# A macaron decoder layer on one core: reversed queries, a sixth weight split behind a copy, spaced squares, running-sum transfers in a new place, and a group add on VectorE

## The chip, the cores and the metric

The kernel runs on one core of a Trainium2 chip. The metric is the device time of one execution in microseconds (us), from the runtime's measurement; the profile, taken from a separate execution of the same program, gives the span from the first to the last instruction. Before the change the median of three runs is 1312.29 us (1311.63 to 1313.32).

The engines are named as the profile names them: PE is the matrix engine (PEld its weight loads), DVE is VectorE, ACT is ScalarE, POOL is GpSimd, and SP issues transfers. ACT and POOL issue transfers too.

## The reference

One layer for a sequence of 512 tokens with 1024 features, in float32:

```
x = x + 0.5 * swiglu(rms_norm(x), ffn1)          # 1024 -> 2 x 2816 -> 1024
x = x + mixer(rms_norm(x))                       # two head groups share projections
x = x + cross_attention(rms_norm(x), mem)        # 4 heads over 256 memory rows
x = x + 0.5 * swiglu(rms_norm(x), ffn2)
out = rms_norm(x) * gain
```

The mixer has 16 state-space (SSD) heads in 4 groups, with a causal convolution, a chunked scan over 4 chunks of 128 tokens, a gate and a norm for each group of 256 features; and 8 differential-attention heads, each with two query-key pairs of 64 features. Their logits get a bias by relative position before a causal softmax:

```
rel  = k_pos[None, :] - q_pos[:, None]
bias = rel_bias[rel_bucket(rel)]                 # depends on k_pos - q_pos alone
logits = q k^T * scale + bias                    # masked where rel > 0
w = softmax(logits[0]) - lam * softmax(logits[1]);  out = w v
```

## The kernel before

**Arithmetic.** Every matrix product is done in a reduced 32-bit format with operands split into a high and a low part: ACT copies the value into the high part (`wh` for weights, L155; with a factor L159), DVE subtracts to get the low part (`wl`, L156; with a factor L160), and PE runs three products (high by high, high by low, low by high). PE is fed by these splits everywhere, and each split of a 128 x 1024 weight tile must be done before the product that uses it. The weight tiles come from a pool with three buffers each for `wh` and `wl` and six for the raw tile `wr`, so a split may also have to wait until an earlier product has released its buffer.

**FFN blocks.** Each FFN is worked in three parts of the hidden dimension ("thirds"). The input projection of a pair of hidden tiles is a 2 x 2 block product done with seven products in place of eight: the function `quad` (L270). It runs the products `11`, S1, S2, `12`, S3, S4 and `22` of 24 matmuls each (2.88 us), into three accumulators `qa`, `qe`, `qb` (`a_ps`, `e_ps`, `b_ps` in the code; L243 issues the matmuls). Between them ACT copies `qa` into `qb` (L287 or L292), `qe` into `p` (L295) and `qb` into `u` (L302), and DVE forms the sums of weights that S2 and `22` need (L297 to L307, where they aren't ready in memory) and `qe - u` (L303). S3 adds into `qb`, so it cannot begin before `u` has been copied out of it. Seven splits of weights feed the seven products; the split for S4 (`w3`, the sixth) comes ahead of that product. The projected activations go through the gate (L450, L453), and a gated pair is combined into `s31` and `s24` (L212 to L214), which are split too (`s31h`, `s31l`, `s24h`, `s24l`) for the output product.

The output projection of a third is `out_blocks` (L1271): the same seven products, in parts of one or two tiles (`part`), into `oa`, `oe`, `ob` (L1300 issues the matmuls, L1311 updates the residual `x`). In the first FFN the sums of weights are not in memory: the function `added` fetches a block through SP and has POOL issue a transfer that adds a second block onto it in place (L1320); `t2` fetches a third block and DVE adds it (L1330); and `t4` has POOL add one more block onto the running sum with a transfer (L1341). In the last third, where `by_dma` is set, all running sums are done so. The raw tile of the first part of S3 is called `gate` there.

**What sets the order.** A scheduler sets the order of PE, DVE and ACT at build time. A class `Order` interleaves the generators of the dense work with spawned chains by estimated times; `yield` gives way to the other chains, and its number is the estimated time until the chain goes on. SP and POOL issue in program order. The helper `behind(list)` makes an instruction come after those listed on the same engine; it adds no wait between engines. An engine executes its instructions strictly in order, so an instruction that waits holds back everything behind it on its engine.

**Attention.** `queries_keys` projects one head's queries and keys and splits them (`split("q", pq, -1.0)` writes `qh` on ACT and `ql` on DVE). The bias of a head is a Toeplitz matrix. The kernel computes one row of it for each head in memory (`rel_d`, 8 rows of 640 values), copies this row 128 times into a second memory tensor `rel_z` with rows one longer (`expand_bias`, L640: two transfers from ACT, six from SP), and then reads it back shifted by one for each partition (`ask_bias`, L738). `head` adds it to the scores in the instruction at L776, and at the end transposes the output into `pot` and splits it into `yah` and `yal` (`split("ya", pt, wsub)`), the operands of the mixer's output projection `pm`, which L863 adds onto `x`.

**SSD groups.** At the end of each of the four groups ACT squares the two gated tiles (`ysq`, L1003), POOL adds the two (L1005), PE sums over the partitions (`pn`), and a chain of small steps (`nv` on DVE, then `ncol`, `ch`, `cl` and `ndiag` on POOL, `nrow` on PE) makes the norm's factors. POOL's queue also holds transfers that build weight sums for the second FFN in memory (L1266).

**The last squares.** Before the second FFN the residual is squared tile by tile on ACT with the row sum accumulated (`junk`, L554, four tiles last), and from the sums the norm's row is made, which the first gates of FFN2 need.

Of the kernel before, what the change touches and what calls it, by code (L numbers as in the profile page):

```python
# [100 lines left out]
def body(tc, a, dbg=None):  # L101
# [81 lines left out]
    @contextmanager  # L183
    def behind(ins):
        with ExitStack() as after:
            for i in ins:
                after.enter_context(tc.issue_after(i))
            yield
# [71 lines left out]
    def quad(xs, src, ready, fresh=False):  # L260
# [40 lines left out]
        u2 = s2("u2")  # L301
        S.activation(u2, b_ps, AF.Copy)  # L302
        V.tensor_tensor(e_ps, e_ps, u2, ALU.subtract)  # L303
# [6 lines left out]
        V.tensor_tensor(c22, p5, b_ps, ALU.subtract)  # L310
        yield from add_product(e_ps, split_w(m3), xs, S4, False)
        yield from add_product(b_ps, split_w(t4), xs, "22", False)
# [283 lines left out]
    rel_d = dram.tile([8, RW], F32, name="rel_d")  # L596
    rel_z = dram.tile([8, P, RW + 1], F32, name="rel_z")

# [18 lines left out]
    def prepare():  # L617
# [14 lines left out]
        hot.clear()  # L632
        yield 6.0
        for hd in range(2):
            with behind(list(recent)):
                expand_bias(S, hd)
            yield 4.0

    def expand_bias(queue, hd):
        queue.dma_start(rel_z[hd, :, :RW], rel_d[hd : hd + 1].to_broadcast([P, RW]))  # L640

# [94 lines left out]
    def ask_bias(hd):  # L736
        biases[hd] = s2("bias")
        S.dma_start(biases[hd], bass.AP(rel_z.tensor, rel_z.offset + hd * P * (RW + 1) + P - 1, [[RW, P], [1, T]]))  # L738

    def queries_keys(hd):  # L740
        if hd == 0:
            ask_bias(0)
        if hd < 7:
            ask_bias(hd + 1)
        if hd < 6:
            expand_bias(nc.sync, hd + 2)
        pq = acc("pq")
        yield from proj(pq, load_w(a["wq"][hd]), h)
        q = split("q", pq, -1.0)
        pk = acc("pk")  # L750
# [4 lines left out]
    def head(hd, q, kq, bias):  # L755
# [93 lines left out]
        for b in range(4):  # L849
            transpose(pt[:, b * P : (b + 1) * P], on[:, b])  # L850
        ya[hd] = split("ya", pt, wsub)
        dump(f"ya_{hd}", ya[hd][0])
# [59 lines left out]
    def group(g, bt, ct, xs, zs):  # L912
# [87 lines left out]
        for j in range(2):  # L1000
# [3 lines left out]
            sq.append(q_)  # L1004
        G.tensor_tensor(sq[0], sq[0], sq[1], ALU.add)  # L1005
        yield W["gq"] + (1.2 if g == 2 else 0.0)
# [262 lines left out]
    def out_blocks(blocks, sums, g, col4, ncol4, each=None, finale=None, clean=True, n=None, by_dma=False):  # L1269
# [109 lines left out]
        for t in range(2):  # L1379
            update(t, 0, a_ps[t])  # L1380
        yield from product(b_ps, sums[1], S3)
        for part in t_raw if by_dma else ():
            t4(part)
        for t in range(2):
# [79 lines left out]
    def turn_last():  # L1464
        yield from turn(1, summed=True)
        od.spawn(row_from(st_2, 8.0), 3.0)

# [91 lines left out]
```

## Time and profile before

| | us |
|---|---|
| median of three runs | 1312.29 |
| profiled execution, its own time | 1312.46 |
| its span, first to last instruction | 1310.7 |
| PE busy | 1287.7 |
| DVE busy | 970.1 |
| ACT busy | 707.8 |
| POOL busy | 127.1 |
| last matmul ends, from the start of the span | 1301.4 |

The profiled execution takes 1.8 us more than its span. PE is busy for all but 23 us of the span: 1.4 us pass before its first matmul, 9.3 us after its last, and the rest lies in gaps of 0.1 to 1.6 us between matmuls. So a change that leaves PE's own work as it is can only move these gaps, or make new ones. The names on both sides of an arrow in the rows below are the program's tiles, and the text in square brackets says how long an engine sat idle before an instruction and which instruction on another engine ended that wait.

### The profile page before, as it was taken

The page shows a single profiled execution, that of the slowest core. Times are in us where ns is not written, and L with a number is a line of the kernel's source. Part 1 is how long each engine was busy: PE and PEld are TensorE (multiplying, and loading weights), DVE is VectorE, ACT ScalarE, POOL GpSimd, SP SyncE. Part 2 cuts the span into 40 slices and gives each one's busy share as a digit, 9 for nine tenths or more (in the row PEclk, how much of TensorE's full clock was granted, in tenths as well). Part 3 has the DMA queues.
Part 4 walks back from the last instruction along what each step waited for, and adds up shares of the span by engine and source line. Part 5 has one row for each costly group of instructions (what it writes and reads, how often), then busy time and mean ns, then how long its engine had stood idle before and what let it go on. Part 6 is the DMA issues. An engine that isn't in the chain of part 4 may idle for free.

```text
span 1310.7 us, 20079 instructions
## 1 busy us (share of the span) xinstructions
PE 1287.7 (98%) x7709; PEld 1123.3 (86%) x7709; DVE 970.1 (74%) x1538; ACT 707.8 (54%) x1208; POOL 127.1 (10%) x153
## 2 busy tenths in 40 slices
PE   9999999999999999999999999999999999999997
PEld 7879998997787778777788878888889999989995
DVE  6977897797775676557867686645668878877886
ACT  7545564565754564346645465434365646555564
POOL 0001010001010011101003022020001000000000
PEclk9999999999999999999999999999999999999999
DMA  9367777776984434763466548684139876656652
GB/s 339 94 171 182 203 192 212 223 200 187 291 294 146 137 65 131 256 171 105 92 185 174 177 138 239 191 222 126 66 100 272 207 232 179 189 194 180 188 200 94
DMA packets 70415, 237.38 MB, mean 181 GB/s; under 512 B 8288, under 2 KB 9792, under 8 KB 69968
## 3 DMA queue, kind: packets, MB, share of 16 engines
q1 hardware_dynamic: 54064, 182.87, 41.1%
q0 software_dynamic: 13168, 45.67, 19.4%
q10 hardware_dynamic: 3088, 7.56, 1.6%
q8 instruction: 60, 0.98, 0.3%
q14 instruction: 35, 0.29, 0.1%
HBM read 233.92 MB, written 50.91 MB: 217 GB/s over the span
## 4 chain that ended last, share of the span: by engine, by line
PE 59%; issue 11%; DVE 3%; ACT 2%; DMA 1%; POOL 1%; POOLq 0%; ACTq 0%; DVEq 0%
PE pm L146 10%; PE qb L243 8%; PE qe L243 5%; PE qa L243 5%; PE pxbc L146 4%; PE ob L1300 4%; PE pcq L146 3%; PE pz L146 3%; PE oe L1300 2%; PE oa L1300 2%; PE pcv L146 2%; PE pq L146 2%; PE pv L146 1%; PE pk L146 1%; DMA gate<-in_f1b 1%
## 5 line engine op out<-in xcount | busy, mean ns | idle before, releaser
L155 ACT ACTIVATE wh<-wr 128x1024 fp32r<-128x1024 f32 (+1 forms) x323 | 328.4, 1020 | 355.7 <-issue 75.6
L156 DVE TENSOR_TENSOR wl<-wr,wh 128x1024 fp32r<-128x1024 f32 (+1 forms) x323 | 377.8, 1173 | 142.4 <-ACT wh L155 136.1
L777 ACT ACTIVATE ec<-ec,mn 128x512 f32<-128x512 f32 (+3 forms) x64 | 35.3, 554 | 33.7 <-DVE mn L776 33.7
L146 PE MATMUL pxbc<-hnh,wh 128*128 128x512 f32 x128 | 52.6, 411 | 0.0
L146 PE MATMUL pxbc<-hnh,wl 128*128 128x512 f32 x128 | 50.2, 393 | 0.0
L146 PE MATMUL pxbc<-hnl,wh 128*128 128x512 f32 x128 | 50.2, 392 | 0.0
L243 PE MATMUL qb<-s31h,wh 128*128 128x256 f32 x152 | 43.2, 284 | 3.2 <-ACT u L302 3.2
L243 PE MATMUL qb<-s24h,wh 128*128 128x256 f32 x152 | 43.1, 284 | 1.3 <-ACT qb L287 1.3
L243 PE MATMUL qa<-h11h,wh 128*128 128x256 f32 x152 | 43.1, 283 | 0.0
L243 PE MATMUL qa<-hmh,wh 128*128 128x256 f32 x152 | 43.0, 283 | 0.0
L243 PE MATMUL qa<-hml,wh 128*128 128x256 f32 x152 | 43.0, 283 | 0.0
L243 PE MATMUL qe<-s24h,wh 128*128 128x256 f32 x152 | 43.0, 283 | 0.0
L243 PE MATMUL qe<-s24l,wh 128*128 128x256 f32 x152 | 43.0, 283 | 0.0
L243 PE MATMUL qe<-s24h,wl 128*128 128x256 f32 x152 | 43.0, 283 | 0.0
L243 PE MATMUL qb<-hmh,wh 128*128 128x256 f32 x152 | 43.0, 283 | 0.0
L243 PE MATMUL qb<-hml,wh 128*128 128x256 f32 x152 | 43.0, 283 | 0.0
L243 PE MATMUL qb<-hmh,wl 128*128 128x256 f32 x152 | 43.0, 283 | 0.0
L243 PE MATMUL qa<-h11h,wl 128*128 128x256 f32 x152 | 43.0, 283 | 0.0
L243 PE MATMUL qb<-s24l,wh 128*128 128x256 f32 x152 | 43.0, 283 | 0.0
L243 PE MATMUL qb<-s24h,wl 128*128 128x256 f32 x152 | 43.0, 283 | 0.0
L243 PE MATMUL qa<-h11l,wh 128*128 128x256 f32 x152 | 43.0, 283 | 0.0
L243 PE MATMUL qa<-hmh,wl 128*128 128x256 f32 x152 | 43.0, 283 | 0.0
(457 smaller groups left out, 4169.9 us busy)
## 6 DMA issues: line engine op xcount, KB each, us to landing
wr<-in_f2q SPq DMA_DIRECT2D x44, 512.0 KB, 4.3
wr<-in_f1q SPq DMA_DIRECT2D x40, 512.0 KB, 4.4
wr<-in_f1b SPq DMA_DIRECT2D x25, 512.0 KB, 5.3
isum<-in_f2q SPq DMA_DIRECT2D x22, 512.0 KB, 5.2
wr<-isum SPq DMA_DIRECT2D x22, 512.0 KB, 5.1
wsum<-in_f2b SPq DMA_DIRECT2D x20, 512.0 KB, 6.2
wr<-wsum SPq DMA_DIRECT2D x20, 512.0 KB, 4.7
wr<-in_f1q POOLq DMA_DIRECT2D x16, 512.0 KB, 5.9
```

The source lines that it names most:

```text
L146: newest_mm[:] = [nc.tensor.matmul(out, w, x, start=start, stop=stop).ins]
L155: S.activation(hi, src, AF.Copy),
L156: V.tensor_tensor(lo, src, hi.bitcast(F32), ALU.subtract),
L243: newest_mm[:] = [nc.tensor.matmul(out, a_[:, wc], b_, start=first and f == 0 and kp == 0 and j == 0, stop=kp == n - 1 and j == 2, skip_gr ...
L777: S.activation(ec[:, :n], ec[:, :n], AF.Exp, bias=mn, scale=-1.0, accum_out=sm[c][:, i : i + 1])
L1300: newest_mm[:] = [nc.tensor.matmul(ps, a_[:, ts], b_[:, ws], start=first and k == 0 and j == 0, stop=k == n - 1 and j == 2, skip_group_che ...
```

## The change

Five things change, and no matmul is added or removed (PE has the same 7333 rows of the program; two short pieces of it stand in another place).

- **Sixth split behind a copy.** In every `quad`, the split of the weights for S4 (`w3`) is now ordered behind the copy `u` on ACT.
- **Reversed queries.** The queries are reversed within each block of 128 as they are split (`backwards`: the split reads its source with a step of -1), and the bias is read from `rel_d` with overlapping rows in one transfer; `rel_z` and its eight expanding transfers go. The attention output is turned back when `pot` is split into `ya`. 8 `qh`, 8 `ql`, 8 `yah` and 8 `yal` instructions read PSUM backwards.
- **Last squares spaced.** The four last squares are a chain of their own, 2 us apart by the planner's estimate and each behind the newest split of weights, in place of four in a row.
- **Running sums' transfers.** In the last third of the first FFN, the `t4` transfers are written inside the product S3, behind that product's first split, and no longer after it.
- **Group squares added on VectorE.** The add at L1005 moves from POOL to DVE, four times.

```diff
--- before.py
+++ after.py
@@ -299,7 +299,7 @@
         if not ready:
             V.tensor_tensor(t4, t2, m2, ALU.add)
         u2 = s2("u2")
-        S.activation(u2, b_ps, AF.Copy)
+        copy = S.activation(u2, b_ps, AF.Copy)
         V.tensor_tensor(e_ps, e_ps, u2, ALU.subtract)
         yield from add_product(a_ps, split_w(m2), xs, "12", False)
         w7 = split_w(m7)
@@ -308,7 +308,9 @@
         yield from add_product(b_ps, w7, xs, S3, False)
         c22 = s2("c22")
         V.tensor_tensor(c22, p5, b_ps, ALU.subtract)
-        yield from add_product(e_ps, split_w(m3), xs, S4, False)
+        with behind([copy.ins]):
+            w3 = split_w(m3)
+        yield from add_product(e_ps, w3, xs, S4, False)
         yield from add_product(b_ps, split_w(t4), xs, "22", False)
         yield (a_ps, b_ps), (e_ps, c22)
 
@@ -594,7 +596,6 @@
     wsub = cp.tile([P, 1], F32, name="wsub")
     dskh = cp.tile([P, 8], F32, name="dskh")
     rel_d = dram.tile([8, RW], F32, name="rel_d")
-    rel_z = dram.tile([8, P, RW + 1], F32, name="rel_z")
 
     def lambdas():
         lamv = cp.tile([P, 4, 64], F32, name="lamv")
@@ -630,14 +631,6 @@
         for i in range(2):
             S.dma_start(rel_d[:, i * H : (i + 1) * H], hot[i][:8])
         hot.clear()
-        yield 6.0
-        for hd in range(2):
-            with behind(list(recent)):
-                expand_bias(S, hd)
-            yield 4.0
-
-    def expand_bias(queue, hd):
-        queue.dma_start(rel_z[hd, :, :RW], rel_d[hd : hd + 1].to_broadcast([P, RW]))
 
     def bc_c(t):
         return t[:, None, :].to_broadcast([P, 4, 16])
@@ -735,18 +728,20 @@
 
     def ask_bias(hd):
         biases[hd] = s2("bias")
-        S.dma_start(biases[hd], bass.AP(rel_z.tensor, rel_z.offset + hd * P * (RW + 1) + P - 1, [[RW, P], [1, T]]))
+        S.dma_start(biases[hd], bass.AP(rel_d.tensor, rel_d.offset + hd * RW, [[1, P], [1, T]]))
+
+    def backwards(t):
+        n = t.free_size()
+        return bass.AP(t.tensor, t.offset + P - 1, [list(t.ap[0]), [P, n // P], [-1, P]])
 
     def queries_keys(hd):
         if hd == 0:
             ask_bias(0)
         if hd < 7:
             ask_bias(hd + 1)
-        if hd < 6:
-            expand_bias(nc.sync, hd + 2)
         pq = acc("pq")
         yield from proj(pq, load_w(a["wq"][hd]), h)
-        q = split("q", pq, -1.0)
+        q = split("q", backwards(pq), -1.0)
         pk = acc("pk")
         yield from proj(pk, load_w(a["wk"][hd]), h)
         kq = split("k", pk)
@@ -848,7 +843,7 @@
         pt = aux("pot")
         for b in range(4):
             transpose(pt[:, b * P : (b + 1) * P], on[:, b])
-        ya[hd] = split("ya", pt, wsub)
+        ya[hd] = split("ya", backwards(pt), wsub)
         dump(f"ya_{hd}", ya[hd][0])
 
     wcv = []
@@ -1002,7 +997,7 @@
             q_ = s2("ysq")
             S.activation(q_, yz[j], AF.Square)
             sq.append(q_)
-        G.tensor_tensor(sq[0], sq[0], sq[1], ALU.add)
+        V.tensor_tensor(sq[0], sq[0], sq[1], ALU.add)
         yield W["gq"] + (1.2 if g == 2 else 0.0)
         pn = aux("pn", (P, 4))
         for b in range(4):
@@ -1378,9 +1373,14 @@
         later.clear()
         for t in range(2):
             update(t, 0, a_ps[t])
-        yield from product(b_ps, sums[1], S3)
-        for part in t_raw if by_dma else ():
-            t4(part)
+        for n, _ in enumerate(product(b_ps, sums[1], S3)):
+            if n == 0:
+                first_split = list(recent)
+            elif n == 4 and by_dma:
+                with behind(first_split):
+                    for part in t_raw:
+                        t4(part)
+            yield
         for t in range(2):
             update(t + 2, 1, b_ps[t], -1)
         if finale is None:
@@ -1462,8 +1462,15 @@
             yield from out_blocks(a[f"f2b{c}"], wsum[c], g, col4, ncol4, *((norm, store) if at_end else (None, None)), clean=c == 0)
 
     def turn_last():
-        yield from turn(1, summed=True)
-        od.spawn(row_from(st_2, 8.0), 3.0)
+        yield from turn(1)
+        od.spawn(row_of_last(), 4.0)
+
+    def row_of_last():
+        for k in range(4, KT):
+            with behind(list(newest)):
+                squared(k, x[k])
+            yield 2.0
+        yield from row_from(st_2, 3.0)
 
     od.add(turn_last())
     od.add(ffn2())
```

ScalarE around the sixth split, in the first FFN, where a gated pair (`s31`, `s24`) is split between a group's products; `wh_2768` belongs to S3, `wh_2802` to S4 and `wh_2830` to `22`. Before:

```order
L155 ACTIVATE wh_2768<-wr_2618 128x1024
L295 ACTIVATE p_488_2685<-qe_2622 128x512
L155 ACTIVATE wh_2802<-wr_2614 128x1024
L155 ACTIVATE s31h_2710<-s_491_2705 128x512
L155 ACTIVATE wh_2830<-wr_2611 128x1024
L302 ACTIVATE u_495_2733<-qb_2623 128x512
L155 ACTIVATE s24h_2749<-s_492_2706 128x512
L155 ACTIVATE gh_2784<-th_2603 128x512
L155 ACTIVATE wh_2880<-wr_2865 128x1024
```

After, the same place (the tile numbers are one lower):

```order
L155 ACTIVATE wh_2767<-wr_2617 128x1024
L295 ACTIVATE p_488_2684<-qe_2621 128x512
L155 ACTIVATE s31h_2709<-s_491_2704 128x512
L302 ACTIVATE u_495_2732<-qb_2622 128x512
L155 ACTIVATE s24h_2748<-s_492_2705 128x512
L155 ACTIVATE wh_2801<-wr_2613 128x1024
L155 ACTIVATE gh_2783<-th_2602 128x512
L155 ACTIVATE wh_2829<-wr_2610 128x1024
L155 ACTIVATE wh_2879<-wr_2864 128x1024
```

The copy `u` moved ahead of the splits for S4 and for `22`, which stood ahead of it before. The same happens once more, in the next but one group, 42 us later; in the changed kernel's other groups, in both FFNs, the sixth split stands behind `u` as well.

ScalarE at the start of the second FFN: the last tiles of `x`, the four squares `junk`, and the first group's copies and splits (`qb<-qa` is the copy ahead of S2). Before:

```order
L155 ACTIVATE s31h_9789<-s_2038_9783 128x512
L155 ACTIVATE s24h_9793<-s_2039_9784 128x512
L554 ACTIVATE junk_9818,squares_230<-x_119 128x512
L554 ACTIVATE junk_9821,squares_230<-x_121 128x512
L554 ACTIVATE junk_9824,squares_230<-x_123 128x512
L554 ACTIVATE junk_9827,squares_230<-x_125 128x512
L287 ACTIVATE qb_9844<-qa_9842 128x512
L295 ACTIVATE p_2068_9908<-qe_9843 128x512
L155 ACTIVATE wh_9942<-wr_9835 128x1024
L155 ACTIVATE wh_9978<-wr_9837 128x1024
L155 ACTIVATE wh_10015<-wr_9840 128x1024
```

After:

```order
L155 ACTIVATE s31h_9780<-s_2038_9774 128x512
L155 ACTIVATE s24h_9784<-s_2039_9775 128x512
L556 ACTIVATE junk_9872,squares_230<-x_119 128x512
L155 ACTIVATE wh_9925<-wr_9818 128x1024
L287 ACTIVATE qb_9827<-qa_9825 128x512
L295 ACTIVATE p_2062_9887<-qe_9826 128x512
L556 ACTIVATE junk_9899,squares_230<-x_121 128x512
L556 ACTIVATE junk_9920,squares_230<-x_123 128x512
L155 ACTIVATE wh_9955<-wr_9820 128x1024
L302 ACTIVATE u_2067_9922<-qb_9827 128x512
L556 ACTIVATE junk_9947,squares_230<-x_125 128x512
L155 ACTIVATE wh_9993<-wr_9823 128x1024
```

One square stands ahead of the copy now instead of four, and a weight split (`wh_9925`, for the product `12`) has come ahead of it; the other three squares and the row made from them are later.

VectorE in the first FFN's last output blocks. `wr_3374<-wr_3374,wr_3493` and `wr_3460<-wr_3460,wr_3517` are `t2`'s additions for the two parts (L1330, in the changed kernel L1325). Before:

```order
L156 TENSOR_TENSOR g11l_3389<-th_3382,g11h_3388 128x256
L212 TENSOR_TENSOR s_597_3392<-th_3382 128x512
L156 TENSOR_TENSOR wl_3464<-wr_3460,wh_3463 128x1024
L213 TENSOR_TENSOR s_598_3393<-s_597_3392,th_3382 128x256
L1330 TENSOR_TENSOR wr_3374<-wr_3374,wr_3493 128x1024
L214 TENSOR_TENSOR s_598_3393<-s_598_3393,th_3382 128x256
L156 TENSOR_TENSOR s31l_3398<-s_597_3392,s31h_3397 128x512
L1330 TENSOR_TENSOR wr_3460<-wr_3460,wr_3517 128x1024
L156 TENSOR_TENSOR s24l_3402<-s_598_3393,s24h_3401 128x512
L1311 SCALAR_TENSOR_TENSOR x_123<-oe_3411,col_68_293,x_123 128x512
L156 TENSOR_TENSOR gl_3406<-th_3382,gh_3405 128x512
L156 TENSOR_TENSOR wl_3497<-wr_3374,wh_3496 128x1024
```

After:

```order
L214 TENSOR_TENSOR s_598_3392<-s_598_3392,th_3381 128x256
L156 TENSOR_TENSOR s31l_3397<-s_597_3391,s31h_3396 128x512
L1325 TENSOR_TENSOR wr_3373<-wr_3373,wr_3492 128x1024
L156 TENSOR_TENSOR s24l_3401<-s_598_3392,s24h_3400 128x512
L1306 SCALAR_TENSOR_TENSOR x_123<-oe_3410,col_68_292,x_123 128x512
L156 TENSOR_TENSOR gl_3405<-th_3381,gh_3404 128x512
L156 TENSOR_TENSOR wl_3496<-wr_3373,wh_3495 128x1024
L160 SCALAR_TENSOR_TENSOR hm_3480<-mem_541_3043,par,hm_3480 128x256
L1306 SCALAR_TENSOR_TENSOR x_125<-oe_3411,col_68_292,x_125 128x512
L160 SCALAR_TENSOR_TENSOR hm_3508<-mem_541_3043,par,hm_3508 128x256
L1325 TENSOR_TENSOR wr_3459<-wr_3459,wr_3516 128x1024
L156 TENSOR_TENSOR wl_3520<-wr_3459,wh_3519 128x1024
```

Both additions moved down: the first behind `s214` and `s31l` (`s_598`, L214, and `s31l`), the second behind two updates of `x` and three splits. The raw tiles that SP and POOL then fetch and add for S3 reuse the buffers these additions release.

## The prediction

> **What bounds the kernel now.** I read the page's busy times first, then the table of what the engines waited for, then the timelines around PE's gaps.
>
> ```profile
> PE 1287.7 (98%) x7709; PEld 1123.3 (86%) x7709; DVE 970.1 (74%) x1538; ACT 707.8 (54%) x1208; POOL 127.1 (10%) x153
> ```
>
> PE is the bound. Of the span of 1310.7 us it is idle for 23.0; since the change takes no matmul away, 23 us is all that could be won, and some 11 of it (the start and the tail) the change doesn't touch. Which waits make the gaps, and where:
>
> ```profile
> PE qb L243 <- ACT u L302: 3.2, 2, 1.6
> PE ob L1300 <- DVE wl L156: 2.4, 3, 1.3
> ...
> PE qb L243 <- ACT qb L287: 1.3, 1, 1.3
> PE pm L146 <- DVE x L863: 1.2, 1, 1.2
> ...
> PE ob L1300 <- ACT wh L155: 0.8, 1, 0.8
> ```
>
> ```profile
> 254.82 0.39 PE L243 MATMUL qb<-s31h,wh 128*128 128x256 f32 x1 [1.58 <-ACT u L302]
> 330.30 0.50 PE L1300 MATMUL ob<-wl,s31h 128*128 128x512 f32 x1 [0.53 <-DVE wl L156]
> 333.70 0.50 PE L1300 MATMUL ob<-wh,s31h 128*128 128x512 f32 x1 [0.82 <-ACT wh L155]
> 334.96 0.50 PE L1300 MATMUL ob<-wl,s31h 128*128 128x512 f32 x1 [0.53 <-DVE wl L156]
> 771.20 0.50 PE L146 MATMUL pm<-yah,wh 128*128 128x512 f32 x1 [1.19 <-DVE x L863]
> 979.70 0.39 PE L243 MATMUL qb<-s24h,wh 128*128 128x256 f32 x1 [1.32 <-ACT qb L287]
> ```
>
> In the first table the columns are the total wait, how many times, and the longest. Four places are touched by the change: the two groups where S3 waits for `u` (3.2 us together), the last output blocks of FFN1 (0.53 + 0.82 + 0.53 = 1.88 us), the third SSD group's end (1.19) and the start of FFN2 (1.32).
>
> **Sixth split behind the copy.** ACT before the first of the two `u` stalls:
>
> ```profile
> 250.33 1.06 ACT L155 ACTIVATE wh<-wr 128x1024 fp32r<-128x1024 f32 x1 [1.33 <-issue]
> 251.30 0.61 ACT L155 ACTIVATE s31h<-s 128x512 fp32r<-128x512 f32 x1
> 253.22 1.06 ACT L155 ACTIVATE wh<-wr 128x1024 fp32r<-128x1024 f32 x1 [1.31 <-PE qa L243]
> 254.19 0.58 ACT L302 ACTIVATE u<-qb 128x512 f32<-128x512 f32 x1
> ...
> 253.97 0.68 DVE L450 TENSOR_TENSOR gate<-qa,row 128x512 f32<-128x512 f32 x1
> 254.57 1.21 DVE L156 TENSOR_TENSOR wl<-wr,wh 128x1024 fp32r<-128x1024 f32 x1
> ```
>
> The split for `22` (at 253.22) waits for the product `12` (`qa`) to release a buffer, and `u`, which needs nothing later than S2, is queued behind it until 254.19. PE ends `12` at 253.24 and resumes 1.58 later. In the new order ACT does `s31h` and then `u`, ahead of both splits: with 0.5 to 0.6 each they are done by about 251.5, 1.7 us before S3 can begin, and `s31l` on DVE is no longer behind the sixth split's low part either. So both stalls go: -3.16. What is late next is the sixth split itself. Its low part now stands on DVE behind the gate that reads `qa` after `12`: 253.24 + 0.7 + 1.2 = 255.2, and S4's product, one S3 of 2.88 us after 253.24, wants it at 256.1: 0.9 us to spare. In two other groups of FFN1's last third, worked out in the same way with these durations, the new order leaves a low part 0 to 0.25 and 0 to 0.15 us late. I take +0.2 for both (0 to +0.4). In the remaining groups the split has a product and more to spare; there it costs nothing, since it runs under 5.76 us of S3 and `12`.
>
> **Last squares spaced.** At the start of FFN2 the copy that S2 waits for stood behind four squares:
>
> ```profile
> 977.24 0.62 ACT L554 ACTIVATE junk<-x 128x512 f32<-128x512 f32 x1
> ...
> 979.07 0.58 ACT L287 ACTIVATE qb<-qa 128x512 f32<-128x512 f32 x1
> 979.59 0.58 ACT L295 ACTIVATE p<-qe 128x512 f32<-128x512 f32 x1
> 980.07 1.99 ACT L155 ACTIVATE wh<-wr 128x1024 fp32r<-128x1024 f32 x2
> ...
> 977.38 0.28 PE L243 MATMUL qa<-h11h,wl 128*128 128x256 f32 x1
> ```
>
> `qa` is complete at about 977.7. One square now stands ahead of the copy, and it is done by then; but a weight split has come ahead too, which needs a buffer that the same product releases. It runs from about 977.7 and lasts 1.0 (1.99 for two), so the copy starts near 978.7 instead of 979.07: -0.35, and no more. Were the split done earlier, the whole 1.32 would go; were it late, nothing would: 0 to -1.3. The row made from the squares comes some 4.5 us later than before, near 992 if its steps keep their distances; the first gates that use it come after `22` of the first group, five products of 2.88 us after 979.3, so near 993.5. Its cover is about 1 us: hidden.
>
> **Group squares on VectorE.**
>
> ```profile
> 768.32 1.29 POOL L1005 TENSOR_TENSOR ysq<-ysq,ysq 128x512 f32<-128x512 f32 x1 [44.80 <-ACT ysq L1003]
> ...
> 767.75 0.69 DVE L156 TENSOR_TENSOR wl<-wr,wh 128x512 fp32r<-128x512 f32 x1 [1.96 <-ACT wh L155]
> 768.67 1.23 DVE L160 SCALAR_TENSOR_TENSOR hm<-mem,par,hm 128x256 fp32r<-128x256 f32 x1 [0.23 <-ACT hm L159]
> 769.82 0.73 DVE L885 SCALAR_TENSOR_TENSOR conv<-pxbc,par,conv 128x511 f32<-128x511 f32 x1
> 770.48 0.67 DVE L863 TENSOR_TENSOR x<-x,pm 128x512 f32<-128x512 f32 x1
> ...
> L160 DVE SCALAR_TENSOR_TENSOR hm<-mem,par,hm x16: 473/478/1225, 318.6 to 768.7; 128x256 fp32r<-128x256 f32 x16
> ```
>
> Four adds of 0.69 each (the row of a 128x512 `wl`) come onto DVE. In three groups nothing on PE's path is behind them. In the third group the order puts the add after the `wl` at 767.75 and ahead of `hm`, `conv` and the `x` for which PE waits. By this alone `x` is 0.61 later less the 0.23 idle: +0.38. But `hm` took 1.23 there, beside the add on POOL, against a median of 0.48 in 16. If POOL's add made it wait, then without it DVE runs add 768.44, `hm` 769.05, `conv` 769.45, `x` 770.11: 0.36 earlier than 770.48. I take -0.36, since only this one of 16 is stretched and only it ran beside that add; bounds -0.36 and +0.38.
>
> The Trainium skill, page "SBUF — State Buffer", section "Who interferes with whom", says that a VectorE instruction with two SBUF inputs contends with a GpSimd instruction that reads SBUF, and that the loser blocks until the other is done. The row agrees: `hm` ends 0.29 after POOL's add (769.61), and by that rule the sum takes the -0.36; by the row's duration alone, taken as `hm`'s own, it would take the +0.38.
>
> **Running sums' transfers, and the queues that lose traffic.** "Behind the first split" orders `t4` against ACT and DVE, but `t4` is issued by POOL, where nothing of the kind stands: its waits are the same and POOL's order there is the same. So that edit by itself does nothing; what changes is what ACT and DVE do around it.
>
> ```profile
> 312.38 1.22 DVE L1330 TENSOR_TENSOR wr<-wr,wr 128x1024 f32<-128x1024 f32 x1
> ...
> 318.10 0.86 POOL L1320 DMA_DIRECT2D wr<-in_f1b  x1 [18.79 <-ACT hot L628]
> 319.31 0.86 POOL L1320 DMA_DIRECT2D gate<-in_f1b  x1 [0.36 <-ACT hm L159]
> ...
> 332.59 1.06 ACT L155 ACTIVATE wh<-gate 128x1024 fp32r<-128x1024 f32 x1 [1.93 <-DMA gate<-in_f1b]
> ```
>
> ```profile
> q0 software_dynamic: 393, 1.48, 53.9%
> q1 hardware_dynamic: 477, 1.76, 41.2%
> q10 hardware_dynamic: 176, 0.34, 6.4%
> ```
>
> The 1.88 us of stalls hang on the transfer `gate`, issued at 319.31 and landed 13.2 us later, while the 16 transfer engines are full (second fence: the queues from 319 to 333, packets, MB, share; q10 carries `rel_z`). Two things act on it. DVE's first addition now stands behind two more instructions (L214's 128x256 and `s31l`, 0.34 + 0.61), so the fetch that reuses its buffer, and the in-place add behind it, go out about 1.0 later: at worst +1.1. And `rel_z`'s 6.4% of the traffic is gone: 0.064 x 13.2 = -0.84 for the landing. Together about +0.2; I take +0.3, as the second addition is later still, and keep -0.9 to +1.2.
>
> The Trainium skill, page "DMA: Bandwidth & Descriptors", section "Queues, rings and completion order", says that a transfer engine goes round its queues a packet at a time, which is nearer to shares by packets than to shares by time. No run here shows yet which of the two holds; by shares of packets the time would be the first rival's.
>
> **Reversed queries.** 8 splits of queries and 8 of `pot` read PSUM with a step of -1; no row shows such a read.
>
> ```profile
> L159 ACT ACTIVATE yah<-pot,wsub x8: 669/677/690, 430.1 to 663.3; 128x512 fp32r<-128x512 f32 x8
> ...
> 622.29 0.68 DVE L160 SCALAR_TENSOR_TENSOR ql<-pq,qh 128x512 fp32r<-128x512 f32 x1
> ...
> 628.52 0.50 PE L146 MATMUL ps<-kh,qh 64*128 64x512 f32 x2
> ```
>
> The shortest distance from a `ql` to the scores that use it is the one shown, 628.52 - 622.97 = 5.5 us. If backward reads took double, `qh` and `ql` would take 1.3 more together, well inside it, and `yah` is not used by PE before the output projection. Bounds 0 to +1 for delays of what is queued behind; I take 0. The bias arrives a head ahead of its use.
>
> **Sum.** -3.16 + 0.2 - 0.35 - 0.36 + 0.3 + 0 = -3.4 us against the profiled execution's 1312.46, which includes 1.8 outside its span and lies 0.17 above the median: 1309.1 by the profile, 1308.9 by the median. I predict 1309.0. A fifth of a per cent, 2.6 us, is about what a measurement of this kernel can tell from no change.
>
> **Rivals.**
> - *The transfers' relief pays in full.* If queues share the engines by packets, `rel_z` took 176 of 1046 of `gate`'s 13.2 us, 2.2, which is more than the delay of 1.0; the stalls at 330 to 335 shrink, by 1.2 or, if the splits before them come earlier too, by all of it, -1.88 in place of +0.3: 1306.8. For it: all queues were full. Against it: q10's first transfer is asked only at 323.6, when `gate` is a third through, and 2.2 less 1.0 covers only 1.2 of the 1.88. Chance 0.12.
> - *The gap moves on.* One of the two `u` stalls comes back as a wait for the sixth split, and the last output blocks lose their full +1.2: -3.4 + 1.58 + 0.9 = -0.9, 1311.4. For it: DVE is behind in both (the gate ahead of the split's low part). Against it: the 0.9 us to spare. Chance 0.22.
> - *Slower: the sixth split is late in every group.* It stands behind `u` now in all 22 groups; if S4 waited d in each, the price would be 22 d. It outweighs the whole gain from d = 0.16 us on, and at d = 0.3 the time is 1309.0 + 6.6 = 1315.6. For it: the two tight groups. Against it: 1 us and more to spare in the others. Chance 0.11.
> - *Forecast*, within about 1.5 of 1309.0: 0.55.
>
> Faster by over 0.2% (below 1309.7): nearly all of the first rival, and 0.5 of the forecast's 0.55, as only a bad region at 330 spoils it: 0.62. Slower: 0.11. Between: 0.27. The range runs from the first rival's 1306.8 to the second's with a little of the unknown costs, 1313.2; it leaves out the slower rival and the ends.
>
> **What would show it.** Right: no wait of PE for `u`; S2 of FFN2's first group waiting 0.9 to 1.0 for `qb`; `hm` at 0.48 beside the third group's add, and the gap before that `pm` at 0.8; the first `gate` stalls at 330 to 335 between 1.5 and 2.5. Wrong: new waits of S4 (`qe`) for `wl`; `qh` and `ql` well above 0.58 and 0.68 with PE waiting for `ps`; the sum of gaps at 305 to 340 above 3.

## The result

| | before | changed |
|---|---|---|
| median of 13 runs, us | 1312.89 | 1310.33 |
| ratio to before, with its 95% interval | | 0.9984 (0.9977 to 0.9991) |
| profiled execution, its own time | 1312.46 | 1310.71 |
| its span | 1310.7 | 1308.9 |
| last matmul ends | 1301.4 | 1299.4 |

The change makes the kernel 2.1 us faster (0.0016 of 1312.9; 1.2 to 3.0 by the interval). The forecast was 3.4 us. The page's busy times after the change, and the table of what PE waited for (total, times, longest):

```profile
PE 1288.9 (98%) x7709; PEld 1123.8 (86%) x7709; DVE 971.9 (74%) x1542; ACT 706.5 (54%) x1208; POOL 119.5 (9%) x149
```

```profile
PE ob L1295 <- DVE wl L156: 1.7, 3, 0.8
...
PE ob L1295 <- ACT wh L155: 1.1, 1, 1.1
...
PE qb L243 <- ACT qb L287: 0.8, 1, 0.8
PE pm L146 <- DVE x L858: 0.8, 1, 0.8
PE oe L1295 <- DVE s31l L156: 0.7, 1, 0.7
...
PE oa L1295 <- DVE g11l L156: 0.4, 1, 0.4
```

The wait for `u`, the largest before, is gone. Two rows are new, the last two of the fence, and the others stand at other places than before, as the timeline of PE shows:

```profile
189.93 0.50 PE L1295 MATMUL oa<-wh,g11l 128*128 128x512 f32 x1 [0.41 <-DVE g11l L156]
194.07 0.50 PE L1295 MATMUL oe<-wh,s31l 128*128 128x512 f32 x1 [0.68 <-DVE s31l L156]
...
317.44 0.50 PE L1295 MATMUL ob<-wl,s24h 128*128 128x512 f32 x1 [0.41 <-DVE wl L156]
321.12 0.50 PE L1295 MATMUL ob<-wh,s24h 128*128 128x512 f32 x1 [1.11 <-ACT wh L155]
...
333.82 0.50 PE L1295 MATMUL ob<-wl,s31h 128*128 128x512 f32 x1 [0.53 <-DVE wl L156]
...
769.68 0.50 PE L146 MATMUL pm<-yah,wh 128*128 128x512 f32 x1 [0.78 <-DVE x L858]
...
977.66 0.39 PE L243 MATMUL qb<-s24h,wh 128*128 128x256 f32 x1 [0.80 <-ACT qb L287]
```

Since both kernels run the same number of matmuls, nearly all in the same order, the start of the n-th matmul of one trace can be set against the n-th of the other. Their difference is called the **lead** here: by how much PE is ahead of the kernel before at that place (all traces are set against the one profile of before). In this profile it goes: -0.6 us in the first loads, -0.1 at 183, -1.6 after the waits at 190 and 194, +1.6 after the two `u` waits have vanished (297), +1.1 after the last output blocks of FFN1 (334), +1.6 after the third SSD group, +2.0 from the start of FFN2 to the end. Two things are not as forecast: about 1.5 us go at 190 to 194, and between 297 and 334 another 0.5 is given back, about half of it already at 298, in S4 of the last group, and the rest in the output blocks.

### The profile page after: what moved, and what is told of

The parts are those of the page before. It is cut to its first block, busy times and chain, and to the rows that moved or that the text cites. A ratio compares the mean times of both kernels' runs of the same rounds, so it can differ in the third digit from the quotient of the medians.

```text
span 1308.9 us, 20080 instructions
## 1 busy us (share of the span) xinstructions
PE 1288.9 (98%) x7709; PEld 1123.8 (86%) x7709; DVE 971.9 (74%) x1542; ACT 706.5 (54%) x1208; POOL 119.5 (9%) x149
## 4 chain that ended last, share of the span: by engine, by line
PE 75%; issue 13%; DVE 4%; DMA 3%; ACT 2%; POOL 1%; POOLq 0%; SPq 0%; ACTq 0%; DVEq 0%
PE qb L243 11%; PE pm L146 10%; PE qa L243 8%; PE qe L243 7%; PE ob L1295 5%; PE pxbc L146 4%; PE pcq L146 3%; PE pz L146 3%; PE oa L1295 3%; PE oe L1295 3%; DMA wr<-in_f1b 2%; PE pa L146 2%; PE pcv L146 2%; PE pg L146 2%; PE pu L146 2%
## 5 line engine op out<-in xcount | busy, mean ns | idle before, releaser
L243 PE MATMUL qb<-s31l,wh 128*128 128x256 f32 x152 | 43.0, 283 | 0.0
L243 PE MATMUL qb<-s31h,wl 128*128 128x256 f32 x152 | 43.0, 283 | 0.0
```

Of the source, the lines that this page charges most:

```text
L243: newest_mm[:] = [nc.tensor.matmul(out, a_[:, wc], b_, start=first and f == 0 and kp == 0 and j == 0, stop=kp == n - 1 and j == 2, skip_gr ...
```

## The experiments

Every kernel below is set against the kernel before, with the same profiles and leads. The lead at 297 is that after both `u` places, the lead at 334 that after the last output blocks of FFN1, and the third column is what was lost between 183 and 197. (At 334 the kernel before still has its last wait there ahead, 0.53 at 335; the seventh-split kernel has no such wait, and its lead at 337 is +3.88. The other leads differ between 334 and 337 by 0.02 at most.)

| kernel | median, us (ratio, interval) | lost at 190 | lead at 297 | lead at 334 | lead at the end |
|---|---|---|---|---|---|
| changed | 1310.33 (0.9984, 0.9977 to 0.9991) | 1.48 | +1.62 | +1.14 | +2.04 |
| changed, second profile | 1311.0 (one run) | 0.00 | +3.12 | +0.77 | +1.74 |
| sixth split alone | 1312.49 (1.0002, 0.9993 to 1.0012) | 1.11 | +2.61 | +0.99 | +1.12 |
| changed without the sixth split's edit | 1310.83 (0.9984, 0.9975 to 0.9993) | 0.22 | -0.30 | +0.48 | +1.43 |
| sixth split in FFN1's last third only | 1308.85 (0.9966, 0.9954 to 0.9979) | 0.01 | +3.04 | +1.81 | +2.84 |
| the same, without its last group | 1309.56 (0.9982, 0.9972 to 0.9991) | 1.32 | +0.08 | +0.95 | +1.75 |
| last third, updates later | 1308.9 (0.9972, 0.9962 to 0.9982) | 1.11 | +2.44 | +1.37 | +2.43 |
| last third, copy first | 1310.62 (one run) | 0.83 | +2.31 | +0.04 | +1.84 |
| reversed queries alone | 1312.3 (one run) | 0.53 | -0.52 | +0.28 | +0.19 |
| seventh split in place of the sixth | 1307.66 (0.9962, 0.9948 to 0.9975) | 0.30 | +2.44 | +3.20 | +4.84 |
| combined | 1306.79 (0.9955, 0.9943 to 0.9968) | 0.35 | +3.21 | +4.79 | +6.62 |

### The sixth split, alone and left out

The first kernel is the one before with the changed kernel's edit in `quad`, and nothing else. The second is the changed kernel with that edit undone:

```diff
-        with behind([copy.ins]):
-            w3 = split_w(m3)
-        yield from add_product(e_ps, w3, xs, S4, False)
+        yield from add_product(e_ps, split_w(m3), xs, S4, False)
```

> The kernel before with the sixth split behind the copy, and nothing else. Theory: that edit alone removes both 1.58 us waits of PE for u, and alone makes the new waits at 189 and 193 us, because a later sixth split releases its raw tile later and so the next third's fetch goes out 1.3 to 1.6 us later; PE loses about 1.5 us there, 0.3 near 272, and the sum is -1.3 to -1.6 us. Rival: the waits at 189 and 193 are scatter of the transfers or come from another part; then they are absent here and the sum is about -2.9.

> The changed kernel with the sixth split where it was before. Theory: both 1.58 us waits for u return, the waits at 189 and 193 go, so 1.3 to 1.6 us slower than the changed kernel, some 0.5 to 0.9 us faster than the kernel before. Rival (scatter, or another part): the waits at 189 and 193 stay, and the time is that of the kernel before plus 0.5 or more.

The edit alone does remove both `u` waits (the lead grows by 1.74 at each of the two places) and yet wins nothing that can be measured: 1.0002, with an interval that begins at 0.9993. The changed kernel without it is as fast as the changed kernel, though it was expected to be 1.3 to 1.6 us slower. So neither the theory's -1.3 to -1.6 nor the rival's -2.9 came about. The largest term of the forecast is worth about zero in the end, and the gain of 2.1 us comes from the other edits. Of the lead of +2.61 at 297, +0.99 is left at 334; in the changed kernel's second profile 3.12 becomes 0.77.

### Only where the waits are

The changed kernel with the sixth split behind the copy in FFN1's last third only (`sixth` is filled for that third and emptied for FFN2):

```diff
-        with behind([copy.ins]):
-            w3 = split_w(m3)
-        yield from add_product(e_ps, w3, xs, S4, False)
+        if sixth:
+            with behind([copy.ins]):
+                w3 = split_w(m3)
+        else:
+            w3 = None
+        yield from add_product(e_ps, w3 or split_w(m3), xs, S4, False)
```

> The changed kernel with the sixth split behind the copy only in the last third of the first feed-forward block, where the two waits for u are. Theory: u waits gone, the waits at 189 and 193 gone too, 1.2 to 1.6 us faster than the changed kernel (about 3.5 us faster than the kernel before). Rival: the waits at 189 and 193 stay and the time is the changed kernel's.

And the changed kernel once more:

> The changed kernel once more, for a second profile. If the waits at 189 and 193 us belong to the sixth split in all groups, they are here again with some 1.0 to 1.5 us; if they are the scatter of the transfers, any value from 0 to 1.5, as the four kernels without that split gave 0 to 0.5 there. The waits at 316 and 320 us belong to the order of instructions and return within 0.2 us.

The kernel of the last third is faster than the changed one by its median (the two intervals still overlap), and shows no wait at 190. By this alone the theory of that place would have seemed right. But the second profile of the changed kernel has no wait there either (its waits at 316 and 320, 0.37 and 1.09, returned as expected), and three kernels further down, which leave the sixth split of the third concerned in its old place, lost 1.32, 1.11 and 0.83: the loss at 190 to 194 runs from 0 to 1.48 over these profiles, whatever the split does. ACT waits there for an in-place add by transfer, and when this lands decides: at 187.11 in the changed kernel's first profile, at 184.89 in its second. The theory falls for this place: it is scatter between executions, and the changed kernel's first profile had a bad draw. What else makes the last-third kernel's median lower was not found.

### What moves the additions

The kernel of the last third again, with the last group's split left where it was (`sixth` is empty for that group, and `late` is true in the last third only):

```diff
         for q in range(nq):
+            sixth[:] = [q] if late and q < nq - 1 else []
```

> The changed kernel with the sixth split behind the copy only in the last third of the first feed-forward block, and there not in its last group. If that group's split is what moves the two additions down on VectorE in the output blocks that follow, both stand again where they stood before, the waits at 316 to 322 us (1.5 us) vanish, those at 330 to 335 are about 1.1, and one wait of 1.58 us for u returns at 295: about the time of split_last_third, within 0.7 us. If the additions' place has another cause, the waits at 316 to 322 stay and it is 1.6 us slower than split_last_third.

The waits at 316 to 322 are gone, and one `u` wait has come back at 295. DVE's two additions, in the changed kernel and in this one:

```profile
313.17 1.22 DVE L1325 TENSOR_TENSOR wr<-wr,wr 128x1024 f32<-128x1024 f32 x1
...
318.75 1.23 DVE L1325 TENSOR_TENSOR wr<-wr,wr 128x1024 f32<-128x1024 f32 x1
```

```profile
312.31 1.22 DVE L1332 TENSOR_TENSOR wr<-wr,wr 128x1024 f32<-128x1024 f32 x1
...
314.38 1.22 DVE L1332 TENSOR_TENSOR wr<-wr,wr 128x1024 f32<-128x1024 f32 x1
```

So it is the last group's split that moves them. (It is not the only edit that can: with the seventh split moved in its place, further down, the second addition is late too, at 316.77.) In the changed kernel without the sixth split's edit, which keeps the new place of the `t4` transfers, they run at 312.68 and 314.75: the `t4` edit has nothing to do with it. The lead at 334 is +0.95 with one `u` wait left, against +1.81, +1.14 and +0.77 in kernels that have removed both: removing the second wait changes it by -0.2 to +0.9, not by 1.6. The time, 0.9982 against the last-third kernel's 0.9966, does not tell the two apart.

To see what the late second addition itself costs, the two updates of `x` that stand ahead of it on DVE were put behind S2 (in `out_blocks`, for the last third of FFN1):

```diff
-        for t in range(2):
-            update(t + 2, 1, e_ps[t], 1, False)
+        if not by_dma:
+            for t in range(2):
+                update(t + 2, 1, e_ps[t], 1, False)
         yield from product(b_ps, sums[2], S2)
+        if by_dma:
+            for t in range(2):
+                update(t + 2, 1, e_ps[t], 1, False)
```

> split_last_third with the two updates of x from oe behind the product S2 in the last output blocks of the first feed-forward block, so that VectorE does the second addition earlier. If the late second addition is the cause of the waits at 316 to 322 us, they shrink from 1.5 to below 0.6, and part of it stays in the end: 0.3 to 1.0 us faster than split_last_third. If the place is bound by the transfer into gate alone, the waits reappear at 330 to 335 and the time is that of split_last_third.

The second addition is at 314.58, and the waits at 313 to 322 shrink from 1.56 to 1.01 (0.21 and 0.80), less than expected. The time is that of the last-third kernel (0.9972 against 0.9966, intervals overlapping): the waits at 328 to 334 take over, 1.31 in all against 0.72.

### Which resource takes the gain back

The `u` waits come from the seventh split (for `22`), which waits for a buffer ahead of `u`; the sixth only stands between. So the seventh can be put behind the copy and the sixth left alone:

```diff
+        yield from add_product(e_ps, split_w(m3), xs, S4, False)
         with behind([copy.ins]):
-            w3 = split_w(m3)
-        yield from add_product(e_ps, w3, xs, S4, False)
-        yield from add_product(b_ps, split_w(t4), xs, "22", False)
+            w4 = split_w(t4)
+        yield from add_product(b_ps, w4, xs, "22", False)
```

> The changed kernel with the seventh split (for the product 22) behind the copy in place of the sixth. Both waits for u were made by the seventh split's wait for a buffer, so they go here too (at most 0.1 left of 3.15). Theory (raw tiles): what takes the gain back in the changed kernel is the sixth split's raw tile, released later, so that the fetches and the last in-place add before the output blocks go out at 300.0 to 301.0 us though the matrix engine is ahead; here that add goes out by 298.5, the waits at 312 to 322 are under 1.0 in all, and the kernel is 0.8 to 2 us faster than the changed kernel. Rival (transfers' throughput): the output blocks end when the transfer into gate has landed, whatever comes before; then the split for gate begins at 331.4 to 332.0 as in the changed kernel, and the time is the changed kernel's within 0.5 us.

It is 5.0 us faster than before (0.9962), and its interval lies just clear of the changed kernel's. The `u` waits vanish here as there; the difference is what happens at the transfers. SP's second fetch in this stretch, the low part of the last group's sixth split on DVE, SP's third fetch, POOL's last in-place add ahead of the output blocks, and ACT's wait for it, in the changed kernel:

```profile
293.71 0.33 SPq L1276 DMA_DIRECT2D wr<-in_f1b  x1
...
297.35 1.22 DVE L156 TENSOR_TENSOR wl<-wr,wh 128x1024 fp32r<-128x1024 f32 x1
...
298.59 0.33 SPq L1276 DMA_DIRECT2D wr<-in_f1b  x1
...
301.03 0.86 POOL L1315 DMA_DIRECT2D wr<-in_f1b  x1 [8.55 <-DVE wl L156]
...
310.00 1.06 ACT L155 ACTIVATE wh<-wr 128x1024 fp32r<-128x1024 f32 x1 [2.52 <-DMA wr<-in_f1b]
```

and with the seventh split behind the copy (without the second fetch, which goes out at 292.28; the last row is DVE's first addition, at 313.17 in the changed kernel):

```profile
293.57 1.22 DVE L156 TENSOR_TENSOR wl<-wr,wh 128x1024 fp32r<-128x1024 f32 x1
...
294.81 0.33 SPq L1276 DMA_DIRECT2D wr<-in_f1b  x1
...
298.79 0.87 POOL L1315 DMA_DIRECT2D wr<-in_f1b  x1 [8.74 <-DVE gl L156]
...
307.45 1.06 ACT L155 ACTIVATE wh<-wr 128x1024 fp32r<-128x1024 f32 x1 [1.03 <-DMA wr<-in_f1b]
...
310.93 1.22 DVE L1325 TENSOR_TENSOR wr<-wr,wr 128x1024 f32<-128x1024 f32 x1
```

The third fetch goes out 0.02 us after the low part of the sixth split has ended, in both (298.57 and 294.79) and in the kernel before too (the low part 293.78 to 295.00, the fetch at 295.02). The sixth split is the last reader of its raw tile `wr`, and the fetch waits for that tile. With the sixth split behind the copy the tile is free 3.6 us later than before though PE is ahead, and the fetch with it.

The theory then has POOL's add held by this fetch, and the traces do not bear that out. In all twelve profiles the add is issued 0.56 us after the landing of the second fetch (issued at 293.71 and landed at 300.47 in the changed kernel), and the `DVE wl` in its brackets only ended at about that time. In the kernel without the last group's edit the third fetch goes out early and the add no earlier than in the changed kernel:

```profile
296.07 0.33 SPq L1283 DMA_DIRECT2D wr<-in_f1b  x1
...
300.95 0.87 POOL L1322 DMA_DIRECT2D wr<-in_f1b  x1 [8.52 <-DVE c L312]
```

What goes with the third fetch is when the add lands:

| kernel | third fetch | add issued | add landed |
|---|---|---|---|
| before | 295.02 | 298.44 | 306.65 |
| last third, without its last group | 296.07 | 300.95 | 306.55 |
| last third | 297.17 | 299.97 | 308.63 |
| changed | 298.59 | 301.03 | 309.89 |
| seventh split in place of the sixth | 294.81 | 298.79 | 307.34 |

In the six profiles with the sixth split moved in the last group the third fetch goes out at 297.10 to 298.59 and the add lands at 308.6 to 310.5; in the other six it is 293.80 to 296.07 and 306.6 to 307.3. In the changed kernel ACT's next split waits for that landing, and the first addition on DVE stands no earlier than before (313.17 against 312.38) though PE is ahead, so PE runs up against the transfers. That the late fetches slow the add because they run beside it fits these rows; no run shows it by itself. Nor is it shown why the second fetch lands later in the seven profiles with the edit in the last third (299.4 to 300.5, against 297.4 to 298.2 in the other five). So the runs show that moving the sixth split costs the gain at this place and moving the seventh does not, and that the raw tile comes free late; the way from there to the late landing is in part argued.

The rival, that the transfers' throughput alone sets the end of the output blocks whatever comes before, falls: `gate`'s split begins at 328.72 here, against 331.45 in the changed kernel, with the same bytes to move. Of the theory's own signs the add's issue (298.79 for 298.5) and the waits at 312 to 322 (1.06 for 1.0) were missed by a little, and the expected 0.8 to 2 us over the changed kernel was low: it is about 2.9 by the ratios. Against the changed kernel without the sixth split's edit (0.9984) it is about 2.9 too, so nearly all of the 3.16 is kept.

### The copy at the start of FFN2

On top of the last-third kernel, the split for `12` behind the copy of `qa`:

```diff
-                S.activation(b_ps, a_ps, AF.Copy)
+                first = [S.activation(b_ps, a_ps, AF.Copy).ins]
...
-        yield from add_product(a_ps, split_w(m2), xs, "12", False)
+        with behind(first if fresh else []):
+            w2 = split_w(m2)
+        yield from add_product(a_ps, w2, xs, "12", False)
```

> split_last_third with the split for the product 12 behind the copy of qa into qb in the second feed-forward block's first group. If that split standing ahead of the copy is what is left of the wait (0.80 us in the changed kernel), the wait falls to 0.1 or less and 0.7 to 0.8 us are won there. If the copy is held by qa's own end, it stays near 0.8.

ACT in the changed kernel, and with this edit:

```profile
976.07 1.06 ACT L155 ACTIVATE wh<-wr 128x1024 fp32r<-128x1024 f32 x1 [0.25 <-PE qa L243]
977.03 0.58 ACT L287 ACTIVATE qb<-qa 128x512 f32<-128x512 f32 x1
```

```profile
977.23 0.58 ACT L289 ACTIVATE qb<-qa 128x512 f32<-128x512 f32 x1 [0.37 <-PE qa L243]
977.73 1.05 ACT L155 ACTIVATE wh<-wr 128x1024 fp32r<-128x1024 f32 x1
```

The wait of PE for this copy is gone, and the lead grows by 1.37 from 973 to 999, against 0.52 in the changed kernel: 0.85 more. Its one run is no faster than the last-third kernel, since this execution lost 0.83 at 190, and S4 waited 0.63 at 298 for the low part of the sixth split: an in-place add for the last group landed late, ACT waited 3.84 for it, and the splits behind it came late too.

### The reversed queries alone

The kernel before with `backwards`, the two splits that use it, the new `ask_bias` and no `rel_z`.

> The kernel before with the reversed queries and the bias read from rel_d alone. Prediction's theory: the splits that read backwards keep 0.58 and 0.68 us; without the expanding transfers the transfer into gate lands 0.8 us earlier after its issue (12.3 instead of 13.2 us), and the three waits at 330 to 335 us (1.88) shrink to about 1.0. Rival, shares by packets: it lands 2.2 us earlier and the three waits shrink to 0.7 or less. Third: it is not the expanding transfers that make it slow, and it lands after 13 us as before.

The transfer into `gate` lands 12.3 us after its issue, and the waits at 330 to 335 go from 1.88 to 1.05:

```profile
330.82 0.51 PE L1293 MATMUL ob<-wl,s31h 128*128 128x512 f32 x1 [0.53 <-DVE wl L156]
...
334.68 0.51 PE L1293 MATMUL ob<-wl,s31h 128*128 128x512 f32 x1 [0.52 <-DVE wl L156]
```

This is the lead from -0.52 at 297 to +0.28 at 334, 0.8 us, and all that this edit gives. The rest of the execution is as before.

### All together

Seventh split, later updates and copy first in one kernel:

> The seventh split behind the copy, the two updates of x behind S2 in the last output blocks, and the second feed-forward block's first copy ahead of the split for the product 12. If the gains add, 0.8 us more than seventh_split from the copy (the wait of 0.80 at 977 goes) and 0 to 0.5 from the updates: 1308 us or less, 4 to 5 us faster than the kernel before. If the copy's gain is taken back by the products that follow, the time is that of seventh_split.

It has the lowest median of all: 1306.79 us, 0.9955 (0.9943 to 0.9968), 5.9 us faster than before; its interval overlaps that of the seventh split. The lead at the end, 6.62, is 1.78 above that of the seventh split: 0.85 from the copy, and most of the rest was there at 297 already (3.21 against 2.44), where the two kernels do the same, so it is scatter. The second addition runs at 311.89 instead of 316.77 and no wait at 319 is left (1.00 in the seventh-split kernel), but from 297 to 337 this wins only 0.15, since the waits for the splits at 326 and 330 (0.29 and 0.53) come in its place.

## Why the prediction was right or wrong

- **Sign and size.** Faster was forecast with -3.4 us, and -2.1 was measured; the time of 1310.33 lies 1.3 above the forecast and within the range. But the parts are not what the sum made of them.
- **Sixth split, -3.16 and +0.2.** Both `u` waits vanish as described. What failed is the sentence "What is late next is the sixth split itself", with its 0.9 us to spare: it looked at the product that reads the split, and not at who waits for the tile that the split reads. The fetch that waits for that tile went out 3.6 us later, the in-place add beside it landed 3.2 us later, and nearly all of the gain was given back: the split alone measured 1.0002, and the term is about 0 instead of -2.96. The rival of the gap that moves on had the right shape, and mostly the wrong wait. The 0.9 us to spare were worked out for the first of the two `u` groups, where PE indeed loses nothing in S4. In the second the low part of the sixth split ends at 298.57 in the changed kernel, and S4's first product with it begins just then:

```profile
298.34 0.28 PE L243 MATMUL qe<-s24l,wh 128*128 128x256 f32 x1
298.62 0.38 PE L243 MATMUL qe<-s24h,wl 128*128 128x256 f32 x1
```

  The lead falls by 0.26 there, in each profile with the edit in that group (0.88 with the copy first), and not at all with the seventh split moved instead. The table of waits has no row for it, since the gap is too short. Another 0.34 is lost at 272; the kernel with the seventh split loses the same there, so that isn't the sixth's low part. The +0.2 was therefore near in size, at another place than the two tight groups.
- **Slower rival.** Of the 22 groups of the changed kernel, S4 loses lead in one, by 0.26 (by 0.88 in the execution with the copy first), far from 22 times 0.16.
- **Running sums' transfers.** That the edit itself does nothing fits: the changed kernel without the sixth split and the kernel with the reversed queries alone have the same additions within 0.25 us. The prediction books the additions' new place under this heading; it comes from the sixth split in the last group. The terms were -0.84 for the traffic, and +1.0 for the delay. The first was right by itself (12.3 against 13.2 us, -0.9; 12.4 and 12.0 in the two other kernels without `rel_z` whose additions stand in the old place). The second was too small: in the changed kernel `gate` was issued 3.4 us later than before (322.72 against 319.31) and landed after 8.6 us. In the first profile the stretch from 297 to 334 lost 0.5, not far from the forecast of +0.3, and in the second 2.35: that the first came out near is luck.

```profile
322.72 0.86 POOL L1315 DMA_DIRECT2D gate<-in_f1b  x1 [2.95 <-ACT wh L155]
...
331.45 1.06 ACT L155 ACTIVATE wh<-gate 128x1024 fp32r<-128x1024 f32 x1 [1.55 <-DMA gate<-in_f1b]
```

- **Shares by packets.** The first rival needed the landing 2.2 us earlier. With the reversed queries alone it was 0.9, which is near the share by time (0.84) and not the share by packets; that q10 was busy in a part of the time only leaves the rule of the page "DMA: Bandwidth & Descriptors" of the Trainium skill neither shown nor refuted.
- **Group squares, -0.36.** Right: PE's wait falls from 1.19 to 0.78. In all three kernels that add on POOL and were profiled, the longest `hm` is 1225 or 1227 ns; in all nine that add on DVE, it is at most 496. The rows of the changed kernel and of the sixth split alone:

```profile
L160 DVE SCALAR_TENSOR_TENSOR hm<-mem,par,hm x16: 476/480/489, 317.3 to 767.8; 128x256 fp32r<-128x256 f32 x16
```

```profile
L160 DVE SCALAR_TENSOR_TENSOR hm<-mem,par,hm x16: 473/479/1225, 316.9 to 767.5; 128x256 fp32r<-128x256 f32 x16
```

  This is what the page "SBUF — State Buffer" of the Trainium skill, section "Who interferes with whom", would have: it says that the loser of such a contention blocks, and the trace agrees.
- **Last squares, -0.35.** Mis-sized a little: the wait went from 1.32 to 0.80, -0.52. That the weight split ahead of the copy holds the rest was shown by putting it behind: the wait vanished.
- **Reversed reads, 0.** Right: the backward reads take as long as the forward ones.

```profile
L159 ACT ACTIVATE qh<-pq x8: 573/582/592, 380.8 to 619.2; 128x512 fp32r<-128x512 f32 x8
L159 ACT ACTIVATE yah<-pot,wsub x8: 672/678/690, 429.0 to 662.2; 128x512 fp32r<-128x512 f32 x8
...
L160 DVE SCALAR_TENSOR_TENSOR ql<-pq,qh x8: 680/684/690, 382.1 to 621.2; 128x512 fp32r<-128x512 f32 x8
```

What stays open: why the in-place add that is issued at 177 to 179 goes out and lands later in some executions (2.2 us between the two of the changed kernel), how the late fetches hold up the add at 300, and how far the places of SP's fetches in other thirds are shifted by the sixth split. The `t4` edit was not run by itself.

## What to carry to other kernels

When an instruction is moved later, ask not only who waits for what it writes, but also who waits for what it reads to be free: in a pool of few buffers the next fetch does. Before an instruction is moved out of the way of another, look which of those ahead really waits; moving that one, and leaving its neighbours where they are, kept the gain here (about 2.9 us by the ratios, where moving the neighbour won nothing). And where a place is bound by transfers, one profile says little: compare two executions of the same kernel before blaming an edit.

## What the runs showed of the hardware

A 128x256 operation on DVE took 1225 to 1227 ns instead of 480 beside a 128x512 add on POOL, once in each of the three profiles where that add ran on POOL, and never in the other nine. Reads of PSUM with a step of -1 cost ACT and DVE nothing measurable (582 and 684 ns, against 582 and 683 forward). And in two executions of the changed kernel the same in-place add by transfer was issued at 176.59 and landed at 184.89, early enough to hide, or was issued at 178.96 and landed at 187.11, late enough that PE lost 1.5 us.
